# Gate and up projections of a feed-forward by one level of Strassen products, in four parts

## The chip, the core and the metric

The kernel runs on one core of one Trainium2 chip. The metric is the device time of one execution in microseconds (us). Engines are called PE (TensorE matmul), PEld (TensorE weight load), DVE (VectorE), ACT (ScalarE), POOL (GpSimd) and SP (SyncE, which here only issues loads and stores).

## The reference, cut to what matters

Two layers over x of 512 tokens and 1024 features, all in float32:

```python
x = x + g1 * (merged @ w_out)                    # three token mixers, gated, before this
h2 = rmsnorm(x, norm2_w) * (1 + sc2) + sh2
x = x + g2 * ((silu(h2 @ w_gate) * (h2 @ w_up)) @ w_down)     # D_FF = 2816
```

`sh1 sc1 g1 sh2 sc2 g2` are six vectors of 1024 from `silu(c) @ w_ada + b_ada` in each layer.

## The kernel before, in words

**Products.** Everything is kept transposed: features on the 128 partitions, 512 tokens in the free dimension, so x is 8 tiles. Each float32 operand is split into two rounded parts, hi and lo, and a product is three matmuls (`mm3`, line 150): hi with hi, hi with lo, lo with hi, all of 512 columns (tokens) and each with its own load of a 128x128 weight block. w_gate and w_up have 8 x 22 blocks each, w_down 22 x 8.

**Weights.** The host lays out all weight blocks in the order of use, in chunks of up to 8 blocks (512 KB). `load_w` (line 212) brings one chunk with one load by SP into `raw` (2 buffers), ACT copies it to `whi` (line 217, 5 buffers), DVE subtracts to get `wlo` (line 220, 5 buffers). `next_w` (line 225) hands out chunks and keeps up to four more in flight. The DVE subtraction is pinned into program order; matmuls are in program order too; other instructions are placed by a list scheduler.

**Order within a layer.** Norm 1; the input projection; pooling, convolution and attention, whose small steps are started by a counter of matmul columns (`tick`, line 126), as are queued DVE tasks (`run_bulk`, at `bulk_rate` of credit for each tick); 24 gate tiles (lines 762 to 808, "the gate stage"); w_out with norm 2 prepared in its tail; then the feed-forward. A dot with w_ada (`ada_step`) is a 512 KB load and one DVE instruction (line 248); 96 of them are needed in both layers, 16 at the start. Of the other 80, 24 are queued in the gate stage of layer 0 at rate 0.45, using the `raw` buffers, and 56 in the first half of its feed-forward at rate 0.75, using `w4` buffers (6, shared with attention).

**Feed-forward before.** Two halves of 11 tiles. In the first, three tiles of gate and three of up are computed "along" (lines 881 to 890), row block by row block as norm 2 delivers the features; the other 19 tiles column by column (`feature_tile`, then `glu`: Silu on ACT, product on DVE, split into hi and lo). After each half come 8 output tiles of w_down over the 11 tiles of that half, each added into x by DVE (`residual`). The last products of each layer (`tail`, line 816) do the last two output tiles in halves of 256 tokens.

**PSUM.** Four tiles `mm` of one bank and two tiles `pair` of two banks.

Of the kernel before, what the change touches and what calls it, by code (L numbers as in the profile page):

```python
# [12 lines left out]
F32 = mybir.dt.float32  # L13
# [24 lines left out]
NF = DFF // P  # L38
FH = NF // 2
EPS = 1e-6  # L40
NEG = -1e30
SCALE = 1.0 / math.sqrt(HD)
C_BLOCKS = 8
FA = 3


# [24 lines left out]
def hybrid_trunk(ctx, tc, xT, ws, ada, cols, pool_w, qk_w, crow, pos, con, out):  # L71
# [77 lines left out]

    def mm3(o, lhs, rhs, start, stop, main=True):  # L150
        matmul(o, lhs[0], rhs[0], start=start, stop=False)
        matmul(o, lhs[0], rhs[1], start=False, stop=False)
        matmul(o, lhs[1], rhs[0], start=False, stop=stop)
# [48 lines left out]

    chunks = deque()
    for l in range(L):
        off = 0
        for blocks in _plan():
            chunks.append((l, off, len(blocks)))
            off += len(blocks) * P * P
    loaded = deque()
    hold = [None]  # L210

    def load_w():
        l, off, n = chunks.popleft()
        raw = wp.tile([P, C_BLOCKS, P], F32, tag="raw", name=nm("raw"), bufs=2)
        nc.sync.dma_start(raw[:, :n], ws[l, off:off + n * P * P].rearrange("(p b n) -> p b n", p=P, n=P))
        hi = wp.tile([P, C_BLOCKS, P], F32R, tag="whi", name=nm("whi"), bufs=5)
        A.activation(hi[:, :n], raw[:, :n], AF.Copy)  # L217
        lo = wp.tile([P, C_BLOCKS, P], F32R, tag="wlo", name=nm("wlo"), bufs=5)
        with tc.issue_after(hold[0].ins) if hold[0] is not None else nullcontext():
            ins = V.tensor_sub(lo[:, :n], raw[:, :n], f32(hi)[:, :n])  # L220
        pin(ins)
        return hi, lo

    def next_w(ahead=4):
        while chunks and len(loaded) <= ahead:
            loaded.append(load_w())
        return loaded.popleft()
# [88 lines left out]
    class Norm:  # L316
# [35 lines left out]
        def apply(self, l, i, k, lo, hi):  # L352
            a = amod[l][i][:, k:k + 1]
            sh = mod[l][:, SH1 if i == 0 else SH2, k:k + 1]
            t = tmp()
            V.scalar_tensor_tensor(t[:, lo:hi], x[k][:, lo:hi], a, self.rstd[:, lo:hi],  # L356
                                   op0=ALU.mult, op1=ALU.mult)
            A.activation(self.hi[k][:, lo:hi], t[:, lo:hi], AF.Identity, bias=sh)
            return V.scalar_tensor_tensor(self.lo[k][:, lo:hi], t[:, lo:hi], sh,  # L359
                                   f32(self.hi[k])[:, lo:hi], op0=ALU.add, op1=ALU.subtract)  # L360

# [214 lines left out]
    for l in range(L):  # L576
# [216 lines left out]
        for step, j in GATE2:  # L793
# [13 lines left out]
            merged.append(split_from(t))  # L807
        if l == 0:
            flush_bulk()

# [4 lines left out]

        def tail(src_of, wblk_of, part, nk, nrm, last, lead=None):

            for n in range(KT - 2):
                o = ps_mm()
                for k in range(nk):  # L820
                    mm3(o, wblk_of(n, k), src_of(k), k == 0, k == nk - 1)
                residual(n, o, 0, S, part)
                if nrm is not None:
                    nrm.add(n, 0, S)
                if last:
                    nc.sync.dma_start(out[n * P:(n + 1) * P, :], x[n])
            for h in range(2):
                c = slice(h * BLOCK, (h + 1) * BLOCK)
                for n in (KT - 2, KT - 1):
                    o = ps_mm()  # L830
                    for k in range(nk):
                        mm3(o[:, :BLOCK], wblk_of(n, k), cut(src_of(k), slice(None), c), k == 0, k == nk - 1)
                    residual(n, o[:, :BLOCK], h * BLOCK, (h + 1) * BLOCK, part)
                    if nrm is not None:
                        nrm.add(n, h * BLOCK, (h + 1) * BLOCK)
                        if h == 1 and n == KT - 2:
                            lead()
                    if last:
                        nc.sync.dma_start(out[n * P:(n + 1) * P, c], x[n][:, c])

        class Blocks:
            def __init__(self, per):
                self.per, self.w = per, {}

            def __call__(self, n, k):
                b = n * self.per + k
                c = b // C_BLOCKS
                if c not in self.w:
                    self.w[c] = next_w(2 if n >= KT - 2 else 4)
                return wblk(self.w[c], b % C_BLOCKS)  # L850
# [8 lines left out]

        n2 = Norm()  # L860
        table(AF.Abs_reciprocal_sqrt, t[:, 0:1])
        bank = ps_pair()[:, 0]
# [5 lines left out]

        for fh in range(2):
            act = []  # L870

            def glu(g, u):
                t = tmp()
                A.activation(t, g, AF.Silu)
                V.tensor_mul(t, u, t)  # L875
                act.append(split_from(t))

            j0 = 0
            if fh == 0:
                j0 = FA  # L880
                held = {}
                for n, (k, lo, hi) in enumerate(HALVES + REST):
# [5 lines left out]
                    for z in range(2 * FA):  # L888
                        mm3(f_ps[z][:, lo:hi], wblk(held[k], z), cut(norm.k(k), slice(None), slice(lo, hi)),
                            k == 0 and lo == 0, k == KT - 1)  # L890
                del held
                for z in range(FA):
                    glu(f_ps[z], f_ps[FA + z])
                if l == 0:
                    bulk.extend(ada_tasks(0, (G2,)))
                    for part in (SC1, SH1, G1, SC2, SH2, G2):
                        bulk.extend(ada_tasks(1, (part,)))
                    bulk_rate[0] = 0.75
            for j in range(j0, FH):
                wg = next_w()  # L900
# [4 lines left out]
                glu(g, u)  # L905
            if fh == 0:
                blk = Blocks(FH)
                for n in range(KT):
                    o = ps_mm()
                    for k in range(FH):  # L910
                        mm3(o, blk(n, k), act[k], k == 0, k == FH - 1)
                    residual(n, o, 0, S, G2)
            else:
                blk = Blocks(FH)
                if l + 1 == L:
                    tail(lambda k: act[k], blk, G2, FH, None, True)
                else:
                    flush_bulk()
                    drain()
                    n1 = Norm()  # L920
                    table(AF.Abs_reciprocal_sqrt, f32(act[-1][1])[:, 0:1])
                    scratch = ps_pair()
                    bank = scratch[:, 1]
                    tail(lambda k: act[k], blk, G2, FH, n1, False, lead(n1, l + 1, 0, bank))
                    norm = n1

# [99 lines left out]
```

## Time and profile before

| | |
|---|---|
| three runs | 1513.8, 1514.62 (median), 1515.72 us |
| the profiled execution | 1513.91 us, span 1512.1 us, granted TensorE clock 1.0 |
| HBM read | 185.34 MB, 124 GB/s over the span |
| instructions on PE | 7251 matmuls, 7251 weight loads |

The profile is of one execution. Its rows name the line, the engine, the operation and tile names without numbers (out<-in), the shapes, a count, busy time and the mean duration in ns. Rows in order of time begin with the start and the duration in us; in brackets stands how long the engine sat idle before, and what released it. A window row gives its bounds, its length, then busy us and instruction count of PE, PEld, DVE, ACT and POOL, the granted clock, the share of the 16 DMA engines and GB/s. Matmuls are pipelined: a row's duration is longer than the distance between two starts.

### The profile page before, as it was taken

Reading aid. Unit: us, or ns where it says so; the run is one execution under the profiler, and the core shown is the slowest. Engines: PE = TensorE matmul, PEld = TensorE weight load, DVE = VectorE, ACT = ScalarE, POOL = GpSimd, SP = SyncE. Lnnn points to the kernel's source line nnn. Section 1 sums busy time; section 2 is a strip of 40 time slices with the busy share of each in tenths; the row PEclk is TensorE's granted clock in tenths of the full one; section 3 lists DMA queues with packets and bytes.
Section 4 is the critical chain, followed back from the end, with each engine's and each line's share of the span. In section 5 each row is a group of like instructions: output and inputs, shape, how many; then the busy total and the mean of one; then the engine's idle time right before and its main releaser. Section 6 shows DMA issues by size and latency. Waiting matters only on the chain.

```text
span 1512.1 us, 18265 instructions
## 1 busy us (share of the span) xinstructions
PE 1499.3 (99%) x7251; PEld 1241.2 (82%) x7251; DVE 852.1 (56%) x1461; ACT 544.3 (36%) x918; POOL 2.1 (0%) x13
## 2 busy tenths in 40 slices
PE   9999999999999999999999999999999999999999
PEld 7887777788888888888888877788888888888888
DVE  7876878646666655653366656665456433233331
ACT  4634554424332212223244344444333322122220
POOL 0000000000000000000000000000000000000000
PEclk9999999999999999999999999999999999999999
DMA  9433533363157666633233321222322333232331
GB/s 350 158 98 125 161 117 113 122 225 105 53 199 241 213 217 212 206 128 98 77 102 95 103 72 58 71 68 84 98 84 72 123 99 98 84 111 87 105 112 46
DMA packets 55013, 188.62 MB, mean 125 GB/s; under 512 B 7056, under 2 KB 7696, under 8 KB 54928
## 3 DMA queue, kind: packets, MB, share of 16 engines
q1 hardware_dynamic: 54208, 186.80, 37.9%
q8 instruction: 57, 0.93, 0.3%
q10 hardware_dynamic: 720, 0.66, 0.1%
q14 instruction: 28, 0.23, 0.0%
HBM read 185.34 MB, written 2.10 MB: 124 GB/s over the span
## 4 chain that ended last, share of the span: by engine, by line
PE 94%; DVE 3%; DMA 1%; ACT 1%; issue 1%; SPq 0%; ACTq 0%
PE mm L142 84%; PE pair L142 8%; PE mm L148 2%; DVE wlo L220 1%; DMA w<-in_ada 0%; DMA x<-in_xT 0%; ACT whi L217 0%; DVE tmp L356 0%; DVE w L248 0%; DMA raw<-in_ada 0%; DMA raw<-in_ws 0%; DVE w L501 0%; DVE raw L248 0%; ACT tmp L486 0%; ACT tmp L484 0%
## 5 line engine op out<-in xcount | busy, mean ns | idle before, releaser
L142 PE MATMUL mm<-big,whi 128*128 128x512 f32 (+1 forms) x3802 | 1124.8, 379 | 5.5 <-DVE big L359 1.8
L142 PEld LDWEIGHTS mm<-big,whi 128*128 128x128 f32 x3802 | 696.4, 188 | 136.4 <-DVE big L359 2.6
L142 PE MATMUL mm<-big,wlo 128*128 128x512 f32 (+1 forms) x1901 | 717.9, 378 | 0.0
L217 ACT ACTIVATE whi<-raw 128x1024 fp32r<-128x1024 f32 (+2 forms) x258 | 268.7, 1042 | 697.6 <-PE mm L142 539.9
L220 DVE TENSOR_TENSOR wlo<-raw,whi 128x1024 fp32r<-128x1024 f32 (+2 forms) x258 | 307.9, 1196 | 268.6 <-ACT whi L217 267.5
L142 PEld LDWEIGHTS mm<-big,wlo 128*128 128x128 f32 x1901 | 357.9, 188 | 66.2
L813 DVE SCALAR_TENSOR_TENSOR x<-mm,mod,x 128x512 f32<-128x512 f32 (+1 forms) x56 | 37.7, 673 | 115.5 <-PE mm L142 115.5
L248 DVE SCALAR_TENSOR_TENSOR w<-w,csil 128x1024 f32<-128x1024 f32 x72 | 86.3, 1218 | 0.2 <-DMA w<-in_ada 0.2
L875 DVE TENSOR_TENSOR tmp<-mm,tmp 128x512 f32<-128x512 f32 x40 | 27.6, 691 | 98.0 <-PE mm L142 98.0
L142 PE MATMUL pair<-whi,big 128*128 128x512 f32 x224 | 76.9, 390 | 0.0
L142 PE MATMUL mm<-whi,big 128*128 128x512 f32 x160 | 57.3, 395 | 1.6 <-ACT big L369 1.3
L383 DVE TENSOR_TENSOR big<-tmp,big 128x512 fp32r<-128x512 f32 x48 | 33.2, 691 | 30.6 <-ACT big L382 30.4
L142 PEld LDWEIGHTS pair<-whi,big 128*128 128x128 f32 x224 | 42.0, 188 | 8.7 <-DVE big L359 0.2
L142 PE MATMUL pair<-wlo,big 128*128 128x512 f32 x112 | 43.7, 390 | 0.0
L500 ACT ACTIVATE w<-mm 128x512 fp32r<-128x512 f32 (+2 forms) x48 | 23.9, 525 | 43.7 <-PE mm L148 43.4
L142 PEld LDWEIGHTS mm<-whi,big 128*128 128x128 f32 x160 | 30.1, 188 | 9.5 <-ACT big L369 1.9
L142 PEld LDWEIGHTS mm<-w,big 128*128 128x128 f32 x240 | 32.4, 190 | 3.8 <-PE mm L142 0.9
L772 DVE SCALAR_TENSOR_TENSOR big<-big,mm 128x512 f32<-128x512 f32 x48 | 32.6, 682 | 5.0 <-PE mm L142 4.0
L142 PE MATMUL mm<-w,big 128*128 128x256 f32 x240 | 34.6, 286 | 0.5 <-DVE big L386 0.5
L382 ACT ACTIVATE big<-tmp 128x512 fp32r<-128x512 f32 x48 | 30.3, 631 | 12.8 <-DVE tmp L667 8.1
L142 PE MATMUL pair<-big,big 64*128 64x256 f32 (+2 forms) x192 | 32.5, 390 | 0.0
L248 DVE SCALAR_TENSOR_TENSOR raw<-raw,csil 128x1024 f32<-128x1024 f32 x24 | 29.3, 1222 | 5.6 <-DMA raw<-in_ada 5.2
(162 smaller groups left out, 876.0 us busy)
## 6 DMA issues: line engine op xcount, KB each, us to landing
raw<-in_ws SPq DMA_DIRECT2D x226, 512.0 KB, 3.6
w<-in_ada SPq DMA_DIRECT2D x72, 512.0 KB, 4.9
raw<-in_ada SPq DMA_DIRECT2D x24, 512.0 KB, 3.8
raw<-in_ws SPq DMA_DIRECT2D x16, 448.0 KB, 3.7
raw<-in_ws SPq DMA_DIRECT2D x16, 384.0 KB, 2.9
x<-in_xT SPq DMA_DIRECT2D x8, 256.0 KB, 5.0
out<-x SPq DMA_DIRECT2D x6, 256.0 KB, 2.0
csil<-in_crow ACTq DMA_DIRECT2D x1, 512.0 KB, 4.5
```

The costliest lines, as they stand in the source:

```text
L142: tc.keep_in_program_order(T.matmul(*a, **k))
L148: tc.keep_in_program_order(T.transpose(*a))
L217: A.activation(hi[:, :n], raw[:, :n], AF.Copy)
L220: ins = V.tensor_sub(lo[:, :n], raw[:, :n], f32(hi)[:, :n])
L248: return V.scalar_tensor_tensor(aw, aw, 1.0, csil, op0=ALU.mult, op1=ALU.mult, accum_out=mod[l][:, part, j:j + 1])
L382: A.activation(hi, src, AF.Copy)
L383: V.tensor_sub(lo, src, f32(hi))
L500: A.activation(ph[dst], tp, AF.Copy)
L772: V.scalar_tensor_tensor(sg, sg, 1.0, branch, op0=ALU.add, op1=ALU.mult)
L813: V.scalar_tensor_tensor(x[k][:, lo:hi], src, mod[l][:, part, k:k + 1], x[k][:, lo:hi], op0=ALU.mult, op1=ALU.add)
L875: V.tensor_mul(t, u, t)
```

## The change

- Of the 22 tiles of gate and up, three are still computed along and one by itself; the other 18 are 9 pairs of neighbouring tiles. For each pair and matrix the 1024 features are two halves (4 row blocks each), the 512 tokens two halves of 256, the two columns the third split: one level of Strassen in Winograd's form, 7 products of 4 row blocks instead of 8. The order of the products on PE is B21 (into a tile e), T4 of the set before, B11, R1, -V, B22, T3; T4 is left pending until after the next set's B21. Three PSUM tiles serve a set: e, a (B11, then -V, T3 and T4 added) and c (R1, then B22 added). Between them ACT copies a out twice and c once (p1, u2, p5), and DVE adds (o1 in two halves, m22).
- Sums of tokens (`make_forms`): T3, R1, -V, T4, from an unrounded copy of h that ACT now also writes in `Norm.apply` (8 tiles `h`); they are made while the along tiles run.
- Sums of weights (`Sums`): two tiles of `w4` for each set. `begin` loads half of each with SP and adds the other operand with an accumulating load from POOL; DVE makes the other two sums. `SUMS_AHEAD` begins them four items ahead. 28 blocks are loaded for a set (16 before) and 28 are split into hi and lo (16 before).
- Feed-forward in four parts of 6, 6, 4 and 6 tiles; w_down after each, so 4 x 8 residuals a layer instead of 2 x 8. The layout in memory is unchanged, so chunks of w_down are put together from up to five loads.
- Dots with w_ada: G1, SC2, SH2 and G2 in the gate stage of both layers (32 each) at rate 0.6, SC1 and SH1 of layer 1 (16) in the first w_down stages of layer 0; none while pairs run.
- The last tail of layer 0 does four output tiles in halves.

The diff, cut to its core:

```diff
+PARTS = ((3, 1, 1), (0, 0, 3), (0, 0, 2), (0, 0, 3))
+SUMS_AHEAD = 4
...
+        def begin(self):
+            self.s12, self.s43 = w4([P, 2, HK * P]), w4([P, 2, HK * P])
+            for dst, other in ((self.s12[:, 0], (1, 1)), (self.s43[:, 1], (0, 0))):
+                nc.sync.dma_start(dst, self.source(0, 1))
+                nc.gpsimd.dma_start(dst, self.source(*other), accum_op=ALU.add)
+        def load(self, sub):
...
+            if sub == 0:
+                self.raw = rawt()
+                fetch(self.raw, self.l, self.blocks(0, 0) + self.blocks(1, 0))
+                pin(V.tensor_add(self.s12[:, 1], self.s12[:, 0], flat(self.raw)[:, 0]))
+                return split_w(self.raw, C_BLOCKS)
+            if sub == 1:
+                pin(V.tensor_add(self.s43[:, 0], self.s12[:, 1], flat(self.raw)[:, 1]))
+                return split_w(blocks(self.s12), C_BLOCKS)
+            if sub == 2:
+                return split_w(blocks(self.s43), C_BLOCKS)
+            raw = rawt()
+            fetch(raw, self.l, self.blocks(1, 1))
+            return split_w(raw, HK)
...
+            if i == 1:
+                A.activation(self.h[k][:, lo:hi], t[:, lo:hi], AF.Identity, bias=sh)
...
-        if l == 0:
-            bulk.extend(ada_tasks(0, (G1, SC2, SH2), True))
-            bulk_rate[0] = 0.45
+        bulk.extend(ada_tasks(l, (G1, SC2, SH2, G2), True))
+        bulk_rate[0] = 0.6
...
+        def make_forms(c):
+            h1, h2 = norm.h[c], norm.h[HK + c]
+            one, two = bigt(F32), bigt(F32)
+            t3, r1 = one[:, :BLOCK], one[:, BLOCK:]
+            nv, t4 = two[:, :BLOCK], two[:, BLOCK:]
+            V.tensor_sub(t3, h2[:, BLOCK:], h1[:, BLOCK:])
+            V.tensor_sub(r1, h1[:, :BLOCK], h1[:, BLOCK:])
+            V.scalar_tensor_tensor(nv, t3, -1.0, h1[:, :BLOCK], op0=ALU.mult, op1=ALU.subtract)
+            V.scalar_tensor_tensor(t4, nv, -1.0, h2[:, :BLOCK], op0=ALU.mult, op1=ALU.subtract)
+            (a, al), (b, bl) = split_from(one), split_from(two)
...
+        def group(o, w, g, name, start):
+            for c in range(HK):
+                mm3(o, wblk(w, 4 * g + c), forms[c][name], start and c == 0, c == HK - 1,
+                    skip_group_check=not start)
...
+        def strassen(use):
+            e, a, c = ps_pair()[:, 0, :BLOCK], ps_mm()[:, :BLOCK], ps_mm()[:, :BLOCK]
+            w = next_w()
+            group(e, w, 1, "B21", True)
+            flush_pending()
+            group(a, w, 0, "B11", True)
+            q1, q2, o1 = tmp(), tmp(), tmp()
+            p1, u2, p5, m22 = q1[:, :BLOCK], q1[:, BLOCK:], q2[:, :BLOCK], q2[:, BLOCK:]
+            A.activation(p1, a, AF.Copy)
+            V.tensor_add(o1[:, :BLOCK], p1, e)
+            w = next_w()
+            group(c, w, 0, "R1", True)
+            A.activation(p5, c, AF.Copy)
+            group(a, w, 1, "-V", False)
+            A.activation(u2, a, AF.Copy)
+            w = next_w()
+            group(c, w, 0, "B22", False)
+            V.tensor_add(o1[:, BLOCK:], u2, c)
+            group(a, w, 1, "T3", False)
+            V.tensor_add(m22, p5, a)
+            w = next_w()
+            def end():
+                group(a, w, 0, "T4", False)
+                use(o1, a, m22)
+            pending.append(end)
...
+            for _ in range(pairs):
+                glu_pair()
+            flush_pending()
+            if part == 0 and l + 1 < L:
+                bulk.extend(ada_tasks(l + 1, (SC1, SH1)))
+            bulk_rate[0] = 0.75
+            blk = Blocks(nk, 4)
...
-                    tail(lambda k: act[k], blk, G2, FH, n1, False, lead(n1, l + 1, 0, bank))
+                tail(lambda k: act[k], blk, G2, nk, n1, False, lead(n1, l + 1, 0, bank), 4)
```

`glu_pair` calls `strassen` twice. For the gate matrix ACT takes Silu of the four quarters; for the up matrix DVE multiplies them in and `split_from` (ACT, DVE) makes the two activation tiles.

More of the change, by code (lines that the diff above doesn't have):

```diff
@@ L38 @@
 NF = DFF // P
-FH = NF // 2
 EPS = 1e-6
@@ L209, in hybrid_trunk, with rawt @@
+    items = []
+    for l in range(L):
+        first_part = [b for b in _plan() if b[0][0] not in ("gate", "up", "down")]
+        for blocks in first_part + list(feed_forward()):
+            if isinstance(blocks, tuple):
+                sums = Sums(l, *blocks)
+                items += [(sums, sub) for sub in range(4)]
+            else:
+                items.append((None, (l, blocks)))
+    at = [0, 0]
     loaded = deque()
     hold = [None]
[L212 to L215, printed above, removed]
+    def rawt():
+        return wp.tile([P, C_BLOCKS, P], F32, tag="raw", name=nm("raw"), bufs=2)
@@ L860, in hybrid_trunk @@
         n2 = Norm()
+        n2.h = [bigt(F32) for _ in range(KT)]
         table(AF.Abs_reciprocal_sqrt, t[:, 0:1])
@@ L881, in hybrid_trunk @@
+        for part, (along, single, pairs) in enumerate(PARTS):
+            act = []
+            nk = along + single + 2 * pairs
+            if along:
                 held = {}
@@ L893, in hybrid_trunk @@
                     glu(f_ps[z], f_ps[FA + z])
[L894 to L899, printed above, removed]
+            for _ in range(single):
                 wg = next_w()
```

171 lines of the change are left out of this document (126 added, 45 removed).

## The prediction

> **What bounds the kernel now.** I read the page's busy times and its chain of waits first, then the PE rows in order of time, then the windows of one feed-forward.
>
> ```profile
> PE 1499.3 (99%) x7251; PEld 1241.2 (82%) x7251; DVE 852.1 (56%) x1461; ACT 544.3 (36%) x918; POOL 2.1 (0%) x13
> ...
> PE 94%; DVE 3%; DMA 1%; ACT 1%; issue 1%; SPq 0%; ACTq 0%
> ```
>
> PE has work in 99% of the span and owns 94% of the chain that ended last. So the time is the number of matmuls times their pitch, plus whatever makes PE wait. The pitch stands in the last 20 us, where the shape changes from 512 to 256 columns with nothing else going on:
>
> ```profile
> 1484.79 0.62 PE L142 MATMUL mm<-big,whi 128*128 128x512 f32 x2
> ...
> 1492.95 0.40 PE L142 MATMUL mm<-big,whi 128*128 128x256 f32 x2
> ...
> 1498.70 0.40 PE L142 MATMUL mm<-big,whi 128*128 128x256 f32 x2
> ```
> ```profile
> 1490.00:1494.00 4.00, 4.00 (x23) 3.49 (x22) 0.75 (x1) 0.00 (x0) 1.00 0.00 0
> 1494.00:1498.00 4.00, 4.00 (x36) 4.00 (x35) 0.48 (x1) 0.00 (x0) 1.00 0.17 66
> ```
>
> From 1484.79 to 1492.95 run 12 triples of 512 columns: 8.16/36 = 0.2267 us each. From 1492.95 to 1498.70 run 16 triples of 256: 5.75/48 = 0.120 us. Half the columns cost 53% of the time, and the second window says why: PEld (second busy column) is full there, so weight loads, one per matmul, set the pace.
>
> **The products.** A plain pair of tiles is 2 x 8 x 3 = 48 matmuls of 512: 48 x 0.2267 = 10.88 us. A Strassen pair is 7 products x 4 row blocks x 3 = 84 matmuls of 256: 84 x 0.120 = 10.08 us. So 12.5% less arithmetic is 0.80 us (7.4%) of PE time. There are 9 pairs x 2 matrices x 2 layers = 36: **-28.8 us**. The tails: before, two of 66 + 132 half matmuls' excess, 2 x (132 x 0.120 - 66 x 0.2267) = 1.76 us; after, 144 x 0.120 - 72 x 0.2267 = 0.96 in layer 0 and 0.48 in layer 1: -0.3 us.
>
> The Trainium skill (TensorE: Matmul & The Clock Gate, section Back-to-back issue gap) gives 518 cycles for 512 columns and 262 for 256 at 2.4 GHz, 216 and 109 ns, almost halves. By it the products would save an estimated 36 x (48 x 0.216 - 84 x 0.109) = 44 us; the rows above differ (227 and 120) and decide here.
>
> **What stands beside PE.** Per Strassen product set, from these rows:
>
> ```profile
> L217 ACT ACTIVATE whi<-raw 128x1024 fp32r<-128x1024 f32 (+2 forms) x258 | 268.7, 1042 | 697.6 <-PE mm L142 539.9
> L220 DVE TENSOR_TENSOR wlo<-raw,whi 128x1024 fp32r<-128x1024 f32 (+2 forms) x258 | 307.9, 1196 | 268.6 <-ACT whi L217 267.5
> ...
> L383 DVE TENSOR_TENSOR big<-tmp,big 128x512 fp32r<-128x512 f32 x48 | 33.2, 691 | 30.6 <-ACT big L382 30.4
> ...
> L382 ACT ACTIVATE big<-tmp 128x512 fp32r<-128x512 f32 x48 | 30.3, 631 | 12.8 <-DVE tmp L667 8.1
> ```
> ```profile
> L740 DVE TENSOR_TENSOR big<-mm,big 128x256 fp32r<-128x256 f32 x8 | 3.3, 417 | 1.5 <-ACT big L739 1.5
> L739 ACT ACTIVATE big<-pair 128x256 fp32r<-128x256 f32 x8 | 3.1, 384 | 3.2 <-DVE big L740 2.4 <-PE pair L142 0.8
> ```
>
> DVE: three lo splits of 1024 (3 x 1.20), one of 512 (0.69), two adds of weights (2 x 0.69), three adds out of PSUM (3 x 0.42), half of the gating (0.69 + 2 x 0.42 + 2 x 0.69, over two): 8.4 us. ACT: 3 x 1.04 + 0.63 of hi splits, three copies of 0.38, 1.3 of Silu or splits: 6.2 us. DVE thus goes to about 81% of a 10.4 us stretch. It fits, but the queue is in order, so waits in it count.
>
> **The wait that the change adds.** The accumulator *a* is written four times (B11, -V, T3, T4), and before -V and before T3 ACT must have copied it out (p1, u2). In the built order of the changed kernel, 28 of the 36 p1 copies and 28 of the 36 u2 copies stand directly behind a hi split of 1024, which waits for PE to give back the buffer that the same group has just read. Lead times:
>
> ```profile
> 369.34 0.62 PE L142 MATMUL mm<-big,whi 128*128 128x512 f32 x2
> ...
> 369.80 0.39 PE L142 MATMUL mm<-big,wlo 128*128 128x512 f32 x1
> ...
> 370.05 1.06 ACT L217 ACTIVATE whi<-raw 128x1024 fp32r<-128x1024 f32 x1 [3.84 <-PE mm L142]
> 370.23 0.75 DVE L813 SCALAR_TENSOR_TENSOR x<-mm,mod,x 128x512 f32<-128x512 f32 x1 [2.16 <-PE mm L142]
> ```
> ```profile
> 118.67 1.06 ACT L217 ACTIVATE whi<-raw 128x1024 fp32r<-128x1024 f32 x1
> 119.62 0.38 ACT L739 ACTIVATE big<-mm 128x256 fp32r<-128x256 f32 x1
> ```
> ```profile
> 399.64 0.48 DVE L359 SCALAR_TENSOR_TENSOR big<-tmp,mod,big 128x256 fp32r<-128x256 f32 x1
> ...
> 400.17 0.39 PE L142 MATMUL mm<-big,whi 128*128 128x256 f32 x1 [0.26 <-DVE big L359]
> ...
> 400.39 0.28 PE L142 MATMUL mm<-big,wlo 128*128 128x256 f32 x1
> ```
>
> The hi split starts 0.09 us after the last matmul that reads hi (369.96 to 370.05); a 256-column copy behind it ends 0.95 + 0.38 = 1.33 us after the split's start; and after a release (400.12) the second matmul starts at 400.39, as if the first had started unhindered at 400.27, so a restart costs 0.15. With a group's start as T: its eleventh matmul (last reader of hi) starts at T+1.20 and, lasting 0.28, ends at T+1.48; the split runs from 1.57, the copy ends at 2.90, PE goes on at T+3.05. The group between lasts to T+2.88. That is 0.17 us lost per copy, 56 times: **+9.5 us**. Bounds: nothing, if ACT puts the copy first in time, to 0.40 each (22 us), if a late sum or DVE holds the split.
>
> At the end of each of 8 parts, T4 follows T3 with no group between. The copy m22 on DVE must come first: T3 ends 0.16 after its 1.44, 0.04 to DVE (370.19 to 370.23 above), 0.42 of add, 0.15 to restart: 0.77 x 8 = **+6.2 us**. Behind it, the last activation tile (gating 0.42, split 0.63 and 0.69) is covered by the other tiles' products, nk - 1 times 0.68 us; only the part with two pairs (2.04 us) is short. And p5 of the last set stands behind a hi split whose weights come as three to five small loads: I take 0.2 each, **+1.6**; bounds 0 and 1 us each.
>
> **The adding loads.** No row of before shows one. A sum is begun one whole set (10.4 us) or more before DVE reads it. Nearest rows:
>
> ```profile
> raw<-in_ws SPq DMA_DIRECT2D x226, 512.0 KB, 3.6
> ```
> ```profile
> 520.00:582.00 62.00, 62.00 (x275) 51.36 (x274) 32.90 (x49) 12.22 (x12) 0.00 (x0) 1.00 0.63 212
> ```
>
> 256 KB plain (at most 3.6 us) and then 256 KB added: bounded below by the same 3.6, above by nothing I can quote; 3.6 to 6.8 us would be hidden, and I take it as hidden. Traffic, 28 blocks of 64 KB in 10.4 us, is 176 GB/s; the window shows 212 with PE full.
> The Trainium skill (DMA: Bandwidth & Descriptors, section Anatomy of one DMA) gives about 2.0 us plus bytes over 436 GB/s for a load issued from GpSimd, an estimated 2.6 us here, which would also be hidden; no run so far shows it.
>
> **Forms, moved dots, more parts.** Forms: per layer 4 x (4 x 0.42 + 2 x 0.69) = 12.2 us of DVE, and 8 more ACT copies. While they are built DVE has this room:
>
> ```profile
> 402.90:436.00 33.10, 32.49 (x187) 28.59 (x186) 20.89 (x31) 16.64 (x24) 0.00 (x0) 1.00 0.43 138
> ```
>
> 20.9 + 12.2 = 33.1 of 33.1 us: full, but the single tile after it (10.9 us) needs no form. I take 0; if that cover were gone, 3 us a layer. The dots with w_ada move into the gate stages: 32 in each layer at a rate of 0.6, where layer 0 had 24 at 0.45 and layer 1 none:
>
> ```profile
> L756 DVE TENSOR_TENSOR big<-mm,big x2: 692/692/692, 131.0 to 877.0; 128x512 f32<-128x512 f32 x2
> ...
> L813 DVE SCALAR_TENSOR_TENSOR x<-mm,mod,x x10: 478/746/751, 359.6 to 400.0; 128x512 f32<-128x512 f32 x6, 128x256 f32<-128x256 f32 x4
> ...
> L813 DVE SCALAR_TENSOR_TENSOR x<-mm,mod,x x10: 479/750/751, 1105.6 to 1146.3; 128x512 f32<-128x512 f32 x6, 128x256 f32<-128x256 f32 x4
> ...
> L248 DVE SCALAR_TENSOR_TENSOR raw<-raw,csil 128x1024 f32<-128x1024 f32 x24 | 29.3, 1222 | 5.6 <-DMA raw<-in_ada 5.2
> ```
>
> From the last convolution product to the first residual is 359.6 - 131.0 = 228.6 us with the 24 dots and 1105.6 - 877.0 = 228.6 without: they cost nothing. A third more still leaves the two `raw` buffers room: 33 weight chunks and 32 dots at about 5.9 us a use (3.6 to land, then 1.04 + 1.20, or 1.22), over two buffers, is 192 of 228 us. I take +1 us for both layers; bounds 0 and 6. The 32 extra residuals (0.75 us each) run on DVE under the next tile's products.
>
> **Sum** against the profiled run: 1513.9 (span 1512.1) - 28.8 - 0.3 + 9.5 + 6.2 + 1.6 + 1 = 1503.1. That run lies 0.7 below the median of 1514.6, so I forecast **1503 us**, -0.8%.
>
> **Rivals.**
> - *The waits eat the gain.* If each of the 56 copies costs 0.35 instead of 0.17 (the hi split itself held up by DVE, 81% full and in order), 10 us more: 1513, no change. For it: both copies sit on one engine behind a split. Against: after p1 (T+2.90) DVE's two adds (0.42 + 0.69) make the split's input by T+4.0, and PE gives back its buffer only at T+4.6.
> - *The adding load is late: slower.* POOL issues two per set, and SP's load, POOL's add, DVE's add, the hi split on ACT and p1 behind it form one line. Once a sum takes over about 10.4 us from begin to landing, each microsecond of lateness returns in all 36 sets: 1 us late is 1503 + 36 = 1539; half of that 1521. Nothing in the trace speaks for it but that it shows no such load.
> - *No copy is late.* ACT is free early and PE runs its seven groups without a gap: 1503 - 9.5 - 1.6 = 1492.
> - *256 columns at half the pitch of 512*, 0.1134 us: a further 36 x 84 x 0.0066 = 20 us, 1483. The skill's page above points this way; the full PEld window speaks against it.
>
> **How the numbers follow.** Forecast (1496 to 1511) 0.50; waits eat the gain 0.14, of which 0.12 lies within 0.2% (about 3 us, what a measurement of this kernel can tell from no change) and 0.02 above; adding load late 0.20; no copy late 0.13; half pitch 0.03. Faster 0.50 + 0.13 + 0.03 = 0.66, same 0.12, slower 0.22. The range, 1490 to 1527, leaves out the half pitch, the lower edge of the case without waits, and adding loads late by more than 0.7 us.
>
> **What would show it.** In the profile after: 256-column triples at 0.36 us inside the Strassen stretches; idle PE of about 0.2 us before -V and T3, put down to ACT copies, and 0.8 before the last T4 of a part, put down to DVE; POOL's queue with 72 loads that land within 7 us; no idle DVE waiting for them; 228 to 230 us for both gate stages. It is wrong if PE's idle time before -V and T3 is well over 10 us in all, if DVE's longest waits are for the adding loads, or if the gate stages grow.

## The result, and the profile after

The changed kernel takes **1538.4 us** (median of four runs, 1536.1 to 1541.2) against 1514.3 for the kernel before: ratio 1.0158, 95% interval [1.0140, 1.0177]. It is 1.6% slower, clear of the noise; the forecast was 1503 us, and the range ended at 1527. The profiled execution took 1541.2 us with a span of 1539.0.

First the page's busy times and its DMA issues. The last column of an issue row is the median time to landing:

```profile
PE 1494.0 (97%) x8523; PEld 1287.6 (84%) x8523; DVE 1040.3 (68%) x1815; ACT 661.6 (43%) x1156; POOL 64.1 (4%) x85
...
raw<-in_ws SPq DMA_DIRECT2D x146, 512.0 KB, 3.4
...
w<-in_ws POOLq DMA_DIRECT2D x72, 256.0 KB, 5.1
```

PE has fallen from 99% of its span to 97%: it waits for 45 us where it waited for 13. Where it does, the same rows as before tell by stage: the two gate stages begin with the product cv[1] (now line 864) and end with the first residual (line 919), and the feed-forward ends with the last residual of its layer.

```profile
L864 DVE TENSOR_TENSOR big<-mm,big x2: 691/692/692, 130.8 to 882.2; 128x512 f32<-128x512 f32 x2
```
```profile
L919 DVE SCALAR_TENSOR_TENSOR x<-mm,mod,x x46: 476/748/751, 364.2 to 768.9; 128x512 f32<-128x512 f32 x34, 128x256 f32<-128x256 f32 x12
```
```profile
L919 DVE SCALAR_TENSOR_TENSOR x<-mm,mod,x x44: 477/750/752, 1119.9 to 1535.5; 128x512 f32<-128x512 f32 x36, 128x256 f32<-128x256 f32 x8
```

The kernel before has, for the two feed-forwards:

```profile
L813 DVE SCALAR_TENSOR_TENSOR x<-mm,mod,x x28: 478/748/752, 359.6 to 764.0; 128x512 f32<-128x512 f32 x20, 128x256 f32<-128x256 f32 x8
```
```profile
L813 DVE SCALAR_TENSOR_TENSOR x<-mm,mod,x x28: 479/750/752, 1105.6 to 1509.0; 128x512 f32<-128x512 f32 x20, 128x256 f32<-128x256 f32 x8
```

So gate stage 0 went from 228.6 to 233.4 us (+4.8), gate stage 1 from 228.6 to 237.7 (+9.1), feed-forward 0 from 404.4 to 404.7 (+0.3), feed-forward 1 from 403.4 to 415.6 (+12.2). These are the 26.9 us between the spans but for 0.5. The products' gain is gone from both feed-forwards, and the gate stages, in which no product was changed, lost 14 us.

PE's waits by releaser (sum, times, longest) name who was late:

```profile
PE mm L147 <- ACT tmp L1029: 10.1, 4, 3.9
PE mm L147 <- DVE tmp L1036: 8.0, 8, 2.0
```

Line 1029 is p5, a copy on ACT, line 1036 is m22, an add on DVE. Each takes 0.4 us. One of the longest waits in order of time, at the end of the first part in layer 1 (rows of PE loads left out):

```profile
1223.72 0.28 PE L147 MATMUL mm<-big,wlo 128*128 128x256 f32 x1
1226.50 1.06 ACT L307 ACTIVATE whi<-raw 128x1024 fp32r<-128x1024 f32 x1 [4.89 <-DMA raw<-in_ws]
1227.46 0.37 ACT L1029 ACTIVATE tmp<-mm 128x256 f32<-128x256 f32 x1
1227.59 1.23 DVE L310 TENSOR_TENSOR wlo<-raw,whi 128x1024 fp32r<-128x1024 f32 x1 [5.29 <-ACT whi L307]
...
1227.88 0.80 PE L147 MATMUL mm<-big,whi 128*128 128x256 f32 x2 [3.88 <-ACT tmp L1029]
```

PE went through R1 and -V without a gap up to 1223.7, so the last of R1, which p5 copies, was done 12 matmuls earlier, at about 1222.6. But p5 stands in ACT's queue behind the hi split of a chunk of w_down, whose products come four chunks later, and that split waited 4.89 us for its load. The short copy inherits the whole lateness of the chunk. After the pause PE runs at half its clock (first busy column PE, then PEld, DVE, ACT, POOL; then the granted clock, the DMA share and GB/s):

```profile
1220.00:1224.00 4.00, 4.00 (x34) 3.80 (x32) 1.55 (x2) 1.37 (x3) 0.23 (x1) 1.00 0.90 167
1224.00:1228.00 4.00, 0.12 (x2) 0.12 (x1) 0.41 (x1) 1.50 (x3) 0.00 (x0) 0.92 0.65 198
1228.00:1231.00 3.00, 3.00 (x15) 3.00 (x16) 0.89 (x2) 1.16 (x2) 0.00 (x0) 0.54 0.32 78
```

The first row hints at why the chunk is late: DMA is 90% busy while it moves only 167 GB/s (the window 520 to 582 of the kernel before: 63% at 212).

### The profile page after: what moved, and what is told of

Read it like the earlier page. It is cut to its first block, busy times and chain, and to the rows that moved or that the text cites. A ratio compares the mean times of both kernels' runs of the same rounds, so it can differ in the third digit from the quotient of the medians.

```text
span 1539.0 us, 22235 instructions
## 1 busy us (share of the span) xinstructions
PE 1494.0 (97%) x8523; PEld 1287.6 (84%) x8523; DVE 1040.3 (68%) x1815; ACT 661.6 (43%) x1156; POOL 64.1 (4%) x85
## 3 DMA queue, kind: packets, MB, share of 16 engines
q1 hardware_dynamic: 77824, 196.25, 38.6%
q0 software_dynamic: 10368, 18.88, 7.6%
## 5 line engine op out<-in xcount | busy, mean ns | idle before, releaser
L147 PEld LDWEIGHTS mm<-big,whi 128*128 128x128 f32 x4362 | 750.7, 191 | 134.6 <-ACT tmp L1029 10.9
L147 PEld LDWEIGHTS mm<-big,wlo 128*128 128x128 f32 x2181 | 416.1, 191 | 44.7
L307 ACT ACTIVATE whi<-raw 128x1024 fp32r<-128x1024 f32 (+3 forms) x258 | 252.6, 980 | 439.9 <-PE mm L147 231.1
L310 DVE TENSOR_TENSOR wlo<-raw,whi 128x1024 fp32r<-128x1024 f32 (+3 forms) x258 | 289.1, 1123 | 172.3 <-ACT whi L307 171.0
L307 ACT ACTIVATE whi<-w 128x1024 fp32r<-128x1024 f32 x72 | 76.3, 1060 | 98.2 <-PE mm L147 69.8
L252 POOL DMA_DIRECT2D w<-in_ws x72 | 62.1, 918 | 1333.0 <-DMA w<-in_ws 458.0
L310 DVE TENSOR_TENSOR wlo<-w,whi 128x1024 fp32r<-128x1024 f32 x72 | 87.8, 1220 | 15.5 <-ACT whi L307 15.5
L147 PE MATMUL pair<-big,whi 128*128 128x256 f32 (+1 forms) x376 | 74.8, 294 | 0.0
L147 PEld LDWEIGHTS pair<-big,whi 128*128 128x128 f32 x376 | 60.4, 191 | 2.2
L147 PE MATMUL pair<-big,wlo 128*128 128x256 f32 (+1 forms) x188 | 55.3, 294 | 0.0
```

The lines of the kernel that those rows point to most:

```text
L147: tc.keep_in_program_order(T.matmul(*a, **k))
L252: nc.gpsimd.dma_start(dst, self.source(*other), accum_op=ALU.add)
```

## The experiments

Each is told against the kernel before on the same chip. "Gate" and "FF" are the stages as above, layer 0 and layer 1, from each profiled execution; a profile can lie a few us beside its median.

| run | median us | ratio to before, 95% interval | gate 0, 1 | FF 0, 1 |
|---|---|---|---|---|
| kernel before | 1514.3 | | 228.6, 228.6 | 404.4, 403.4 |
| changed kernel | 1538.4 | 1.0158 [1.0140, 1.0177] | 233.4, 237.7 | 404.7, 415.6 |
| contig | 1536.9 | 1.0137 [1.0121, 1.0153] | 234.4, 237.6 | 407.0, 408.5 |
| nodots1 | 1526.5 | 1.0077 [1.0056, 1.0098] | 233.9, 228.6 | 403.2, 406.9 |
| noadd | 1519.6 | 1.0033 [1.0020, 1.0047] | 230.5, 234.4 | 401.1, 402.6 |
| plainparts | 1528.4 | 1.0082 [1.0065, 1.0099] | 233.5, 236.3 | 404.4, 403.9 |
| dotsonly | 1527.5 | 1.0076 [1.0061, 1.0091] | 233.1, 234.9 | 404.5, 404.4 |
| raw3 | 1514.4 | 0.9998 [0.9989, 1.0007] | 232.7, 232.6 | 400.7, 400.4 |
| order | 1528.5 | 1.0091 [1.0076, 1.0106] | 233.7, 237.9 | 401.7, 404.6 |
| all3 | 1520.6 | 1.0035 [1.0022, 1.0047] | 232.7, 232.3 | 404.0, 404.9 |
| early | 1528.8 | 1.0092 [1.0078, 1.0105] | 234.9, 238.5 | 403.8, 402.5 |
| raw3early | 1510.1 | 0.9966 [0.9953, 0.9979] | 230.8, 232.1 | 397.1, 399.1 |
| dots2 | 1540.3 | 1.0165 [1.0151, 1.0179] | 227.9, 227.8 | 427.7, 405.2 |
| cand | 1513.0 | 0.9988 [0.9979, 0.9997] | 228.0, 228.6 | 412.4, 394.3 |
| cand2 | 1504.2 | 0.9928 [0.9915, 0.9942] | 232.9, 229.1 | 397.8, 394.4 |
| **b11** | **1498.2** | **0.9893 [0.9880, 0.9907]** | 231.1, 228.9 | 395.5, 391.8 |
| cand2noadd | 1500.1 | 0.9906 [0.9893, 0.9920] | 231.6, 229.2 | 395.8, 394.3 |
| raw3noadd | 1510.1 | 0.9973 [0.9962, 0.9985] | 231.0, 232.4 | 399.4, 397.4 |

### The gate stages: is it the dots?

**nodots1** leaves out the dots of layer 1's gate stage alone:

```diff
-        bulk.extend(ada_tasks(l, (G1, SC2, SH2, G2), True))
+        if l == 0:
+            bulk.extend(ada_tasks(0, (G1, SC2, SH2, G2), True))
+        else:
+            for part in (G1, SC2, SH2, G2):
+                V.tensor_copy(mod[1][:, part], mod[0][:, part])
+            V.tensor_copy(amod[1][1], amod[0][1])
```

> Layer 1's gate stage computes no dots with w_ada (32 left out, layer 0's four vectors are copied instead, so layer 1 is modulated by the wrong vectors); layer 0's gate stage keeps its 32 and is the control. Theory C (dots that share the two raw buffers with the weight chunks make the chunks late near the end of the gate stage): gate stage 1 goes from 237.7 to 228.6 us (228 to 230), gate stage 0 stays at 233 to 234, the feed-forwards stay: 1538 - 9 = 1529. If something else lengthened the gate stage (more tiles held in the big pool, the new order of chunks), it stays at 236 to 238 and the time at 1536 to 1541.

Gate stage 1 came to 228.6 us, to the tenth what it was before the change, and its control stayed at 233.9. What was not expected: feed-forward 1, which the edit leaves alone, went from 415.6 to 406.9 us in this profile, the fastest of the four runs, in which the granted clock was 1.00 to the end of that stage. So a feed-forward time from one profile can move by several us without a change in it. **dotsonly** makes the opposite test, the kernel before with only the dots moved:

```diff
-        if l == 0:
-            bulk.extend(ada_tasks(0, (G1, SC2, SH2), True))
-            bulk_rate[0] = 0.45
+        bulk.extend(ada_tasks(l, (G1, SC2, SH2, G2), True))
+        bulk_rate[0] = 0.6
...
-        if l == 0:
-            flush_bulk()
+        flush_bulk()
...
-                    bulk.extend(ada_tasks(0, (G2,)))
-                    for part in (SC1, SH1, G1, SC2, SH2, G2):
+                    for part in (SC1, SH1):
```

> The kernel before with nothing of the change but its dots with w_ada: 32 in each gate stage at the rate 0.6, and only 16 for layer 1 in layer 0's feed-forward. Theory C (the dots and the weight chunks share two raw buffers): gate stages of 231 to 235 us in layer 0 and 234 to 237 in layer 1, the feed-forwards unchanged at 404: 1514 + 8 to 13 = 1522 to 1527. If the dots alone cost nothing and the adding loads, which POOL issues as early as 304 us, are what lengthens the gate stages: 229 and 229, 1514.

It lost 12.7 us (the median) without any Strassen product, 10.8 of them in the two gate stages of its profile. The dots alone are more than a third of the 35 us by which the forecast missed. How they cost is seen in the changed kernel at the end of gate stage 1; the load of the last dot, then the lo split of a chunk, the dot, and the next chunk:

```profile
1094.93 0.33 SPq L377 DMA_DIRECT2D raw<-in_ada  x1
```
```profile
1098.33 1.23 DVE L310 TENSOR_TENSOR wlo<-raw,whi 128x1024 fp32r<-128x1024 f32 x1 [3.42 <-ACT whi L307]
...
1099.47 1.22 DVE L353 SCALAR_TENSOR_TENSOR raw<-raw,csil 128x1024 f32<-128x1024 f32 x1
...
1103.14 1.06 ACT L307 ACTIVATE whi<-raw 128x1024 fp32r<-128x1024 f32 x1 [4.36 <-DMA raw<-in_ws]
...
1106.72 0.73 PE L147 MATMUL mm<-big,whi 128*128 128x512 f32 x2 [1.99 <-DVE big L879]
```

The last dot, its load and its wait on DVE held one of the two `raw` buffers from 1094.9 to 1100.7. So the next chunk could only be loaded when the lo split before it gave the other buffer back, at 1099.6, and it landed at 1103.1. Its lo split stood in DVE's queue ahead of the gating (line 879) that PE needed, and PE stood for 2 us, then ran at half clock. The number of dots in a gate stage (24 or 32) and their rate (0.45 or 0.6) were changed together; no run parts the two.

### The ends of the parts: four theories

**contig** lays w_down out in the order of the four parts, so that each chunk is one load:

```diff
+    for along, single, pairs in PARTS:
+        nk = along + single + 2 * pairs
+        down = [("down", k0 + k, n) for n in range(KT) for k in range(nk)]
+        seq += [down[i:i + C_BLOCKS] for i in range(0, len(down), C_BLOCKS)]
+        k0 += nk
```

> Only the order of w_down in DRAM changes: each chunk of 8 blocks that the four parts read is one piece of 512 KB instead of three to five small ones. Theory A (the hi split of a chunk that lands late in pieces stands in ACT's queue ahead of p5, and its lo split ahead of m22 on DVE; PE's pauses then halve its clock): the pauses before B22 at the ends of parts go, those before T4 fall to 0.67 us, and the doubled matmul pitch goes out of both feed-forwards. Feed-forward = 385.1 of PE at pitch + 4.6 of waits on p1 and u2 + 3.1 on m22 + the 3.4 that the kernel before loses too = 396 us, from 404.7 and 415.6: 1538 - 28 = 1510 us (1506 to 1518). Theory B (the adding loads are late or take the queues): less than 6 us gained, the pauses stay, 1532 to 1538. Theory C (the dots with w_ada in the gate stages): no change here. The gate stages stay at 233 and 238 in any case.

Theory A fell, the time hardly moved. The pauses ahead of B22 (p5) did go, but the same us came back ahead of T4. The waits on m22 are now

```profile
PE mm L147 <- DVE tmp L1036: 18.9, 8, 3.4
```

and DVE's own rows show one of the eight (start, duration):

```profile
1327.58 0.69 DVE L1056 TENSOR_TENSOR tmp<-tmp,tmp 128x512 f32<-128x512 f32 x1
1330.07 1.23 DVE L310 TENSOR_TENSOR wlo<-raw,whi 128x1024 fp32r<-128x1024 f32 x1 [1.79 <-ACT whi L307]
1331.21 0.41 DVE L1036 TENSOR_TENSOR tmp<-tmp,mm 128x256 f32<-128x256 f32 x1
```

PE had finished T3 at about 1328.5. m22 stood behind the lo split of a late chunk. So the pieces are not what makes the chunk late; whole chunks are late too.

**noadd** leaves out the adding loads and nothing else:

```diff
-                nc.gpsimd.dma_start(dst, self.source(*other), accum_op=ALU.add)
```

> The 72 adding loads from POOL are left out (the sums lack one block, so the products are of the wrong weights); all other loads, adds, splits and matmuls stay. Theory A (w_down in pieces): the SP loads have less beside them and land a little earlier, the pauses at the ends of parts mostly stay: 2 to 10 us less, 1528 to 1536. Theory B (the adding loads are late, or hold up the rest): the pauses go, both feed-forwards come to 396 us, 1510. If the adding loads cost nothing: 1536 to 1541.

Between the two theories: 19 us went, among them 6 us in the gate stages of this profile, where POOL begins its adding loads already:

```profile
304.48 1.00 POOL L252 DMA_DIRECT2D w<-in_ws  x1 [237.54 <-DMA w<-in_ws]
```

Those 6 us can't all be put down to the adding loads: dotsonly and plainparts (below) have the same 32 dots and no adding load either, and their gate stages are 233.1 and 234.9, 233.5 and 236.3 us, close to the changed kernel's. In the changed kernel no wait of DVE or ACT is put down to a load of a sum. The adding loads harm what lands beside them: at the end of the first part of layer 1 the loads into `raw` took (min, median, max)

```profile
DMA to landing us min/median/max: 3.2/5.5/6.1
```

in the changed kernel and

```profile
DMA to landing us min/median/max: 2.7/3.0/3.1
```

in noadd (three loads against six). This is local: over the whole run a load of 512 KB lands after 3.4 us in the median in both. **raw3** keeps the adding loads and gives the chunks a third buffer, for which it gives up a tile of `big` (46 instead of 47) and two small ones:

```diff
-        return wp.tile([P, C_BLOCKS, P], F32, tag="raw", name=nm("raw"), bufs=2)
+        return wp.tile([P, C_BLOCKS, P], F32, tag="raw", name=nm("raw"), bufs=3)
```

> The changed kernel with three raw buffers in place of two (paid for with one tile of the big pool and two small ones). Theory D (a chunk is late because its load waits for one of two raw buffers, held by the dots in the gate stage and by pieces of w_down at the end of a part): gate stages of 229 to 231, the pauses ahead of T4 at 0.7 to 1 and those ahead of B22 gone, feed-forwards of 396 to 399: 1538 - 4 - 8 - 25 = 1501 (1497 to 1512). Theory E (the landing itself takes too long beside the adding loads, whatever the number of buffers): 1528 to 1538, with the pauses at the ends of parts still 1.5 to 4 us.

Theory D holds for the larger part: the feed-forwards are at 400.7 and 400.4, 24 us went, and the time is that of the kernel before. It falls 13 us short, about half of it in the gate stages, which only came down to 232.7 and 232.6, and half in the feed-forwards, where at four ends of a part the copy u2 is now the one that is late (0.5 to 2.4 us). All eight waits on m22 are now short, at 0.7 us of idle PE each:

```profile
PE mm L147 <- DVE tmp L1036: 5.5, 8, 0.7
...
PE mm L147 <- ACT tmp L1031: 4.1, 4, 2.2
```

**raw3noadd** does both:

> The changed kernel with three raw buffers and without the adding loads (weights wrong). If buffers and adding loads are two handles on one lateness of the chunks: 1505 to 1513, a little under three buffers alone (1514.4). If they are two causes that add up (-19 and -24): 1494 to 1498.

1510.1: 4 us under three buffers alone, not 19. Adding loads and two buffers are two handles on one lateness.

**plainparts** has plain products in the same parts (`PARTS = ((3, 3, 0), (0, 6, 0), (0, 4, 0), (0, 6, 0))`):

> All 22 gate and up tiles as plain products in the same four parts, with w_down in the same pieces, the same dots and the forms still built, but no sums and no Strassen products. If the Strassen sets save what their pitch says less their waits (per layer 18 x 0.80 = 14.4, less 4.6 + 3.1 and less the pauses that stand behind them), and the pieces hurt only because p5 and m22 stand behind them: feed-forwards of 404 to 408 us, gate stages as in the changed kernel, 1514 + 14 + 0 to 8 = 1528 to 1536. If the pieces make PE wait in any case: over 1540. If the sets themselves lose: 1528 with feed-forwards at 404, and the changed kernel's extra time is all in the sets.

Feed-forwards of 404.4 and 403.9, as before the change: four parts, loads in pieces and 32 extra residuals cost nothing where there are no Strassen sets, so neither short copies behind the splits nor adding loads. The total of 1528.4 fits the third case and the edge of the first, so it doesn't choose between them. It does show that in the changed kernel the sets, with all that comes with them, lose 10 us against plain products.

### What stands ahead of the copies

**order** puts the copies first in the queues. The next chunk is fetched after them (`more`), and hi split and copies are pinned:

```diff
-            A.activation(p1, a, AF.Copy)
+            pin(A.activation(p1, a, AF.Copy))
             V.tensor_add(o1[:, :BLOCK], p1, e)
-            w = next_w()
+            more()
+            w = take()
...
-            V.tensor_add(m22, p5, a)
-            w = next_w()
+            pin(V.tensor_add(m22, p5, a))
+            more()
+            w = take()
```

> The changed kernel with the same loads, buffers and products; in the Strassen sets the copies p1, p5, u2 on ACT and m22 on DVE are put ahead of the next chunk's hi and lo split in the in-order queues (the split is issued one group later). Theory F (what PE loses in the sets is the place of these small copies behind a split): the 0.17 and 0.10 us ahead of -V and T3 go (9 us in 36 sets), the pause ahead of B22 goes, that ahead of T4 is 0.77 at each of 8 ends: feed-forwards of 391 to 393 if the chunks of w_down are then in time, 1538 - 36 = 1502; up to 1515 if PE then waits for the chunk itself at the first products with w_down. The gate stages stay at 233 and 238. If nothing of this matters because the chunk is needed at once: 1530 to 1538.

Most of the waits inside the sets went as forecast; left are one pause of 2.8 us ahead of T4 and six new ones of 0.5 to 0.6 us ahead of a part's first B22. But the gain is 10 us, not 36: the late split now stands ahead of the next thing, the split of the last activation tiles (line 502) that the first products with w_down read.

```profile
1398.66 1.06 ACT L308 ACTIVATE whi<-raw 128x1024 fp32r<-128x1024 f32 x1 [6.43 <-DMA raw<-in_ws]
1399.62 0.61 ACT L502 ACTIVATE big<-tmp 128x512 fp32r<-128x512 f32 x1
```

**all3** joins contig, raw3 and order:

> Three raw buffers, w_down in whole chunks of 512 KB and the copies ahead of the splits, all together. If the three are the causes: gate stages of 229 to 230, feed-forwards of 391 to 393, 1538 - 13 - 37 = 1488 us (1484 to 1497), under the kernel before by 1.7%. If the adding loads keep the chunks late in any case: 1505 to 1525.

1520.6 is a miss by 33 us of the first case; it lies in the second (1505 to 1525), and is 6 worse than raw3 alone. As in order, PE waits at the first products with w_down (3.2 us at 644, 3.4 at 1397). I take it that fetching a group later makes the chunks later still; no run parts order from contig with three buffers.

### A cover for the end of a part

**early** runs products with w_down before and after the last T4, and **raw3early** does so with three buffers:

```diff
+            def begin_down(n):
+                o = begun[n] = ps_mm()
+                for k in range(nk - 2):
+                    mm3(o, blk(n, k), act[k], k == 0, False)
+            begin_down(0)
             flush_pending()
+            begin_down(1)
...
```

> The changed kernel with one edit at the end of each part: the first products with w_down (tile 0, all but the last two activation tiles) run before the last T4, those of tile 1 right after it. Theory G (PE's pause before the last T4 is only DVE's m22 with nothing to cover it): the 10.3 us of pauses ahead of T4 go and most of the waits at the first products with w_down; the pauses ahead of B22 (11.4 us) and the gate stages stay: 1538 - 11 = 1527 (1522 to 1533). If PE then waits as long for the chunk of w_down itself, because the chunk is what is late: 1535 to 1540.

> The same edit with three raw buffers. With three buffers alone 7.6 us of pauses ahead of T4 are left, and 1514.4 us. If the chunks are now in time, the pauses go: 1507 (1503 to 1511). If the pause only moves to the first products with w_down: 1512 to 1516.

Both as theory G has it, a little short in the second: -9.5 us against the changed kernel, -4.3 against raw3.

### The rest, and a version that beats both

**dots2** and **cand** spread the dots anew; **cand2** does it more mildly, with raw3, contig and early in it:

```diff
-        bulk.extend(ada_tasks(l, (G1, SC2, SH2, G2), True))
-        bulk_rate[0] = 0.6
+        bulk.extend(ada_tasks(l, (G1, SC2, SH2, G2) if l == 0 else (SC2, SH2, G2), True))
+        bulk_rate[0] = 0.6 if l == 0 else 0.45
...
-                bulk.extend(ada_tasks(l + 1, (SC1, SH1)))
-            bulk_rate[0] = 0.75
+                bulk.extend(ada_tasks(l + 1, (SC1, SH1, G1)))
+            bulk_rate[0] = 1.0
```

> The changed kernel with the dots spread otherwise, none left out: 24 in layer 0's gate stage at the rate 0.45 as in the kernel before, 8 beside the first products of layer 0's feed-forward, 32 beside its products with w_down, and 16 in layer 1's gate stage at 0.3. Theory C: gate stages of 229 and 229 (less if the adding loads that start at 304 us are half of it: 231 and 229), 1538 - 12 = 1526. If the 24 added dots in layer 0's feed-forward make its chunks later, that stage grows from 404.7 to 408 or more, and the time is 1530 or more.

> Three raw buffers, w_down in whole chunks, the early products with w_down and the dots spread as in dots2. If the causes found so far add up: gate stages of 229 (from 232.7 with three buffers), feed-forwards of 395 to 397 (from 400 with three buffers alone): 1514 - 8 - 9 = 1497 (1491 to 1505), 1.1% under the kernel before. If the dots moved into the feed-forward cost there what they save in the gate stages: 1505.

> Three raw buffers, w_down in whole chunks, the early products with w_down, and the dots in a milder spread: 32 in layer 0's gate stage at 0.6, 24 beside layer 0's products with w_down at 1.0, 24 in layer 1's gate stage at 0.45. If the forecast's terms for the products and their waits hold once the lateness is repaired: gate stages of 231 and 228.6, feed-forwards of 397 and 398 us as the earlier runs had them one by one: 1500 to 1502 (1497 to 1507). If the 24 dots beside w_down cost as much as the 40 did (12 us): 1512.

With 24 dots or fewer in it, at a rate of 0.45 or less, a gate stage takes 228 to 229 us, with adding loads or without. But dots2 and cand missed, at 1540 against 1526 and 1513 against 1497: with 24 more dots feed-forward 0 grew by 23 us in dots2. Of these 5.2 us are one pause of PE at 407.8, where four dots in a row, 1.2 us each, stand in DVE's queue ahead of the norm 2 step that PE needs. The dots also use the `w4` buffers of the sums; what that adds to the other 18 us is not shown. cand2 has 8 more dots there and pays nothing that can be seen; it came to 1504.2 us, within its range. **b11** adds one exchange, B11 before B21; **cand2noadd** takes the adding loads out of cand2:

```diff
-            group(e, w, 1, "B21", True)
-            flush_pending()
             group(a, w, 0, "B11", True)
+            flush_pending()
...
             A.activation(p1, a, AF.Copy)
+            group(e, w, 1, "B21", True)
```

> cand2 with B11 computed before B21 in each set, so that p1's copy has two or three groups of products to finish instead of one. If the 0.17 us ahead of -V is the wait on p1 behind a hi split: it goes from 34 sets (0.27 us with u2's share, of which u2's stays), 4 us less than cand2: 1497 (1493 to 1503). If PE waits there for something else, no change against cand2.

> cand2 without the 72 adding loads (the sums lack one block, so the weights are wrong). If the adding loads did harm only through chunks that were late anyway: within 3 us of cand2. If they cost time of their own (they hold the DMA engines twice as long per byte as plain loads): 6 to 15 us less than cand2.

b11 is 1498.2 us, 1.1% under the kernel before, and 6 under cand2; in the profiles 4.9 of that is in the feed-forwards, where the wait ahead of -V is gone. Without the adding loads cand2 would be 4 us faster, between the two cases of the expectation: what is left of their price. The page of b11 has PE back at 99%:

```profile
PE 1475.9 (99%) x8523; PEld 1278.9 (86%) x8523; DVE 1041.0 (70%) x1815; ACT 658.6 (44%) x1156; POOL 64.0 (4%) x85
```

## Why the prediction was wrong, point by point

For the last column I took, in the trace of the changed kernel, how much later than 0.2267 or 0.120 us each matmul starts after the one before, and put it down to the group of products that was late; what the kernel before loses in the same place is taken off. The first row is the number of matmuls of each width in the traces at these two prices.

| step | forecast | measured |
|---|---|---|
| products and tails | -29.1 | -29.6 (counted) |
| p1, u2 | +9.5 | +8.1, and 1.9 once behind a late chunk |
| m22, ends of parts | +6.2 | +10.3 |
| p5, ends of parts | +1.6 | +11.5 |
| outside the sets, mostly the first products with w_down | 0 | +5.0 |
| half clock in the feed-forwards | not named | +5.3 |
| gate stages | +1 | +13.9 |
| sum of these | -10.8 | +26.4 |

- **Products: right.** 256 columns cost 0.120 us inside the sets too; a triple starts every 0.36:

```profile
1222.04 0.40 PE L147 MATMUL mm<-big,whi 128*128 128x256 f32 x2
...
1222.40 0.40 PE L147 MATMUL mm<-big,whi 128*128 128x256 f32 x2
```

  b11 says that most of the gain is there to be had: its two feed-forwards are together 20 us under those of the kernel before.
- **p1 and u2: right, in mechanism and size.** A p1 that stands behind a split costs 0.17 us. Rows of a set late in layer 1:

```profile
1451.74 1.06 ACT L307 ACTIVATE whi<-w 128x1024 fp32r<-128x1024 f32 x1
...
1452.70 0.36 ACT L1025 ACTIVATE tmp<-mm 128x256 f32<-128x256 f32 x1
...
1453.12 0.51 PE L147 MATMUL mm<-big,whi 128*128 128x256 f32 x2
```

  u2 costs 0.17 in a part's first set and 0.11 later. b11 took p1's wait away alone.
- **m22: right where nothing is late** (0.77 forecast; 0.76 to 0.77 from start to start at three ends of a part in the changed kernel, 0.93 to 0.95 at all eight in raw3), too small where a lo split of a late chunk stands ahead.
- **p5: the step that failed in the feed-forwards.** I took 0.2 us with a bound of 1, and no row stood behind either. The place was right, a hi split of w_down ahead of p5 on ACT; the split's own lateness was priced far too low: at four of the eight ends p5 cost 1.5 to 4 us, at the others next to nothing. At the end of a part every chunk goes through `raw`, while in the sets half of them come from `w4`, and the next part's adding loads run at the same time: landings of 5.5 us instead of 3.0, one after the other through two buffers.
- **Adding loads hidden: half wrong.** My rival asked only whether DVE would wait for them (5.1 us to landing in the median, inside the 3.6 to 6.8 I had taken as hidden). It doesn't. What they slow is the plain load next to them, and a rival for that was missing. By the page's queue rows 18.88 MB of them took 7.6% of the engines' span and 196.25 MB of SP's loads 38.6%, twice the engine time for a byte:

```profile
q1 hardware_dynamic: 77824, 196.25, 38.6%
q0 software_dynamic: 10368, 18.88, 7.6%
```

  The 2.6 us that I had estimated from the Trainium skill (DMA: Bandwidth & Descriptors, section Anatomy of one DMA), from a formula for a load issued from GpSimd, are half of the 5.1 measured.
- **Gate stages: the other step that failed.** I took +1, bounds 0 and 6, from a mean: 192 us of use in 228 us of two buffers. That sum took 5.9 us for a dot too, where its own rows give 3.6 + 1.22 = 4.8; with these it is 174 us, 76%. But three quarters of a buffer pair in the mean is not room for each chunk: while a dot and its load hold one buffer, the next chunk can only be loaded when the other comes free. The 24 dots that cost nothing before ended at 334.4 us, 25 us before the first residual; the 32 in layer 1's gate stage end at 1099.5, 20 us before.

```profile
L248 DVE SCALAR_TENSOR_TENSOR raw<-raw,csil x24: 1209/1224/1227, 137.8 to 334.4; 128x1024 f32<-128x1024 f32 x24
```
```profile
L353 DVE SCALAR_TENSOR_TENSOR raw<-raw,csil x32: 1211/1219/1227, 885.5 to 1099.5; 128x1024 f32<-128x1024 f32 x32
```

- **Forms hidden: right.** The first products of a feed-forward have the same three pauses (0.8, 0.5, 0.8 us) as before.

What stays open: why feed-forward 1 loses 9.7 us ahead of B22 and feed-forward 0 only 1.8, with the same instructions; no run sets the phase of the loads by itself. The last 2.5 us in b11's gate stage 0 are, by their size, two pauses of 1.1 and 1.5 us in which PE waits for a step of the attention on DVE (line 599):

```profile
PE mm L153 <- DVE tmp L599: 2.6, 2, 1.5
```

cand2noadd has them too (3.1 us), so they are not the adding loads; no run says whether they come from the 32 dots or from the third buffer.

## What to carry to other kernels

Price a short copy on an in-order queue by the lateness of what stands ahead of it, not by that instruction's duration; then ask at the ends of stages, where prefetch changes its pace, whether that can be late. A buffer pair that is in use for three quarters of the time in the mean can lack the room for one more user. Curing one victim of a late chunk (p5, then m22, then the activation tiles) only hands the wait to the next; what helped was to have the chunk in time (a third buffer) or to give PE other work (early products).

## What the runs showed of the hardware

A pause of PE of about 2 us can halve its clock for some 3 us after it. At the end of gate stage 1, after the 2 us shown above, the granted clock was

```profile
1108.00:1111.00 3.00, 3.00 (x8) 2.32 (x7) 2.91 (x4) 1.50 (x3) 0.00 (x0) 0.50 0.11 41
```

and 512 columns took 0.43 us. In the changed kernel all four pauses that cost over 2 us were followed by it, and of the shorter ones only two close together (at 1115 and 1116); in nodots1 pauses of 2.8 and 3.5 us were not either, so length alone doesn't decide. The clock records of the 18 traces, past the first 140 us, say more. Except for the one that the end of the program cuts off, every stretch at half clock lasts 3.41 us or twice that, and within a trace they all begin on one grid of 3.41 us. In every cell of that grid in which PE stood idle for 1.94 us or more, the clock was halved in the next cell. Under 1.4 us that was so only where it was halved already, and in between it went both ways. The pause of 3.5 us in nodots1 fell on two cells, with 1.6 and 1.7 us. The Trainium skill (TensorE: Matmul & The Clock Gate, section HAM oscillation — how this bites in real kernels) warns of gaps over some 3.4 us; here shorter ones were enough.
